# An offset of its own, from 0 to 480 bytes, for the high and low parts of each seven-block weight chunk

## The chip, the cores and the metric

The kernel runs on one core of a Trainium2 chip. The metric is the device time of one execution in microseconds (us); shorter is better.

## The reference

The reference is a small encoder trunk: 512 tokens of width 1024 in float32, two layers, each an attention and an MLP, and a final RMSNorm.

```python
for layer in range(DEPTH):                       # DEPTH = 2
    hn = rmsnorm(h, norm_mix[layer])
    if layer % 2 == 0:
        h = h + hybrid_attention(hn, ...)        # grouped-query and latent heads
    else:
        h = h + neighbourhood_attention(hn, ...) # an 8 x 16 window, learned bias
    h = h + sq_relu_mlp(rmsnorm(h, norm_ffn[layer]), ffn_w_up[layer], ffn_w_down[layer])
return rmsnorm(h, final_norm)

def sq_relu_mlp(h, w_up, w_down):                # 1024 -> 4096 -> 1024
    u = jax.nn.relu(h @ w_up)
    return (u * u) @ w_down
```

The change is in the MLP of both layers.

## The kernel before

*Products in two parts.* TensorE multiplies in a faster float32 form (`fp32r` in the profile) that keeps fewer bits. So each factor is split into a high part (a copy in that form) and a low part (the rest), and a product is three matmuls: high by high, high by low, low by high. The helper `mm3` (lines 614 to 616) does that for plain products with 512 moving columns.

*Seven blocks.* For much of the MLP the kernel saves multiplications by a scheme of Strassen's kind: a 2 x 2 arrangement of blocks is multiplied by seven block products in the place of eight. `seven_chunk` prepares the weights for it: a DMA on SP's queue brings 256 rows by 256 columns (256 KB) into a raw buffer, GpSimd (in a few chunks VectorE) makes sums and differences of its four 128 x 128 blocks (lines 364 to 366), so that seven wanted blocks lie side by side in columns 128 to 1023 of the buffer. Then ScalarE copies these 896 columns into the high part (line 370, tile `whi`), and VectorE subtracts that from the raw columns into the low part (line 371, tile `wlo`). The raw buffer is a slot of the pool `big` (named `a` in the profile) if enough are free, or a tile `raw` of the pool `wp`.

*Its use.* `Seven.run` goes through the chunks of a product. For each of the seven blocks it runs three matmuls of 128 x 128 weights by 256 moving columns (lines 458 to 460): high weights by high input, high weights by low input, low weights by high input. TensorE loads the weights anew for each. The blocks are taken in the order of the list `SEVEN`, block `a` of the chunk being columns 128 a to 128 a + 127 of `whi` and `wlo`.

*Buffers.* `whi` has three buffers of 1024 columns (4096 bytes in each partition), `wlo` four. Plain chunks (`chunk`, lines 224 and 234) and chunks whose low part a DMA sums (`summed_chunk`) take their parts from the same rings.

*Order.* `weights(i)` hands out the parts of chunk i, and before that asks for loads up to five chunks ahead and for the split up to two chunks ahead (`LOAD`, `AHEAD`). So the high and low part of a chunk are written while TensorE works on the chunks before it, and ScalarE may write the next high part as soon as TensorE is through with the chunk three before. GpSimd's sums are held in program order; the rest of the order on the engines follows the program's text and a planner, which knows nothing of offsets within a tile.

*Who reads and writes what.* The moving input of these matmuls (the parts of the seven combinations of the activations) lies in slots of `big`; the output goes to PSUM. Nothing but lines 370, 371 and 458 to 460 touches the high and low parts of a seven-block chunk.

Of the kernel before, what the change touches and what calls it, by code (L numbers as in the profile page):

```python
# [9 lines left out]
F32R = mybir.dt.float32r  # L10
I32 = mybir.dt.int32
AF = mybir.ActivationFunctionType
ALU = mybir.AluOpType
# [5 lines left out]
P = 128  # L19
# [11 lines left out]
def f32(ap):  # L31
    return ap.bitcast(F32)
# [3 lines left out]
def encoder_kernel(ctx: ExitStack, tc: tile.TileContext, ins, out, dbg=None):  # L36
    nc = tc.nc
    PE, ACT, DVE, POOL, SP = nc.tensor, nc.scalar, nc.vector, nc.gpsimd, nc.sync
# [3 lines left out]
    wp = ctx.enter_context(tc.tile_pool(name="wp", bufs=3))  # L42
# [19 lines left out]
    def nm(s):  # L62
        cnt[0] += 1
        return f"{s}_{cnt[0]}"
# [204 lines left out]
    def rows(w, k0, nk):  # L269
        return w[k0 * P : (k0 + nk) * P, :].rearrange("(k p) n -> p k n", p=P)  # L270
# [16 lines left out]
    def begin(i):  # L287
        while begun[0] < len(loaded):
            make = asked[begun[0]][0]
            if make is summed_chunk and begun[0] > i + SUM:  # L290
                break
            if make in (summed_chunk, seven_chunk):
                next(loaded[begun[0]])
            begun[0] += 1
# [55 lines left out]
    SEVEN = [(0, 0), (2, 2), (4, 5), (3, 3), (5, 4), (6, 1), (1, 6)]  # L350

    reserve = [3]

    def seven_chunk(w, k0, c0, eng=None):


        slot = Slot(F32) if len(free) > reserve[0] else None
        raw = slot.t if slot else wp.tile([P, 1024], F32, tag="raw", bufs=4, name=nm("raw"))
        SP.dma_start(raw[:, 0:512].rearrange("p (k n) -> p k n", k=2), rows(w, k0, 2)[:, :, c0 : c0 + 256])
        r = raw.rearrange("p (b n) -> p b n", n=P)  # L360
        yield
        held = (lambda z: z) if eng else tc.keep_in_program_order
        eng = eng or POOL
        held(eng.tensor_tensor(r[:, 6], r[:, 0], r[:, 1], op=ALU.subtract))
        held(eng.tensor_tensor(r[:, 4:6], r[:, 2:3].to_broadcast([P, 2, P]), r[:, 0:7:6], op=ALU.add))  # L365
        held(eng.tensor_tensor(r[:, 7], r[:, 3], r[:, 5], op=ALU.subtract))  # L366
        yield
        hi = wp.tile([P, 1024], F32R, tag="whi", name=nm("whi"))
        lo = wp.tile([P, 1024], F32R, tag="wlo", bufs=4, name=nm("wlo"))
        ACT.activation(hi[:, 0:896], raw[:, 128:1024], AF.Copy)  # L370
        DVE.tensor_tensor(lo[:, 0:896], raw[:, 128:1024], f32(hi[:, 0:896]), op=ALU.subtract)  # L371
        if slot:
            slot.free()
        yield hi, lo, []

    class Seven:
# [63 lines left out]
        def plan(self, w, c0, pairs=None):  # L440

            return [plan(w, pairs[kp] if pairs else 2 * kp, c0, DVE if pairs and c0 and kp in (2, 5) else None,
                         make=seven_chunk)
                    for kp in range(self.np)]
# [1684 lines left out]
```

## Time and profile before

| | us |
|---|---|
| median of 3 runs | 1156.11 |
| lowest and highest | 1155.82, 1156.34 |
| the profiled execution | 1156.15 |
| its span, first to last instruction | 1154.4 |
| TensorE busy in it | 1144.5 |
| VectorE, ScalarE, GpSimd busy | 894.5, 668.7, 597.4 |

"Busy" is the time in which at least one instruction runs on the engine; TensorE's matmuls are pipelined, so that two that overlap count once, and the row of one matmul gives its own length (start to its modelled end), not its pace. The pace is the distance between two starts. PE is TensorE's matmuls, PEld its weight loads, DVE VectorE, ACT ScalarE, POOL GpSimd, SP the queue from which most DMAs are issued. In a group's row stand line, engine, operation, out<-in by the program's names, the shapes, the count, then busy us and mean ns of one, then the engine's idle time before it and what ended most of that. Where one line of the code is asked for, the three numbers are the shortest, the median and the longest in ns, then the first and last start.

### The profile page before, as it was taken

How to read it: one execution, taken by the hardware profiler on the slowest of the kernel's cores; microseconds unless marked ns; L12 is line 12 of the kernel's file. 1: busy time of each engine (PE TensorE's matmuls, PEld its weight loads, DVE VectorE, ACT ScalarE, POOL GpSimd, SP SyncE). 2: the span in 40 equal slices, each digit the busy share in tenths (PEclk: the TensorE clock that was granted, in tenths of full speed). 3: DMA queues.
4: the chain of work that ended last, by engine and by line, in shares of the span. 5: the costliest groups of instructions: out<-in, count | busy, mean ns of one | idle time of the engine just before them, and what ended most of it. 6: DMA issues, size and time to landing. Idle time of an engine off the chain costs nothing.

```text
span 1154.4 us, 20506 instructions
## 1 busy us (share of the span) xinstructions
PE 1144.5 (99%) x7348; PEld 1032.2 (89%) x7348; DVE 894.5 (77%) x1570; ACT 668.7 (58%) x1133; POOL 597.4 (52%) x722
## 2 busy tenths in 40 slices
PE   9999999999999999999999999999999999999997
PEld 8787888888899999899988998988889999989996
DVE  6887998888968777978775667668996877698774
ACT  6676886756256668544454556546543666773334
POOL 4456532327698882378433232321487889436730
PEclk9999999999999999999999999999999999999999
DMA  7322441122523325923585564343343233372332
GB/s 237 109 77 71 120 110 56 64 68 100 180 74 93 91 84 155 268 93 101 153 167 158 150 168 128 117 117 115 114 146 119 75 101 90 72 188 72 120 119 73
DMA packets 118326, 136.06 MB, mean 118 GB/s; under 512 B 9924, under 2 KB 99953, under 8 KB 118225
## 3 DMA queue, kind: packets, MB, share of 16 engines
q1 hardware_dynamic: 110736, 119.83, 34.0%
q0 software_dynamic: 7312, 14.83, 6.7%
q8 instruction: 58, 0.95, 0.3%
q14 instruction: 44, 0.35, 0.1%
q10 hardware_dynamic: 176, 0.10, 0.0%
HBM read 112.70 MB, written 6.29 MB: 103 GB/s over the span
## 4 chain that ended last, share of the span: by engine, by line
PE 93%; issue 4%; DVE 2%; ACT 1%; POOL 0%; POOLq 0%; DVEq 0%; ACTq 0%
PE mm L614 9%; PE mm L615 9%; PE mm L616 9%; PE mm L460 4%; PE mm L459 4%; PE mm L458 4%; PE t L460 3%; PE t L459 3%; PE t L458 3%; PE s L1139 3%; PE o L1127 2%; PE s L460 2%; PE s L459 2%; PE s L458 2%; PE s L616 2%
## 5 line engine op out<-in xcount | busy, mean ns | idle before, releaser
L371 DVE TENSOR_TENSOR wlo<-a,whi 128x896 fp32r<-128x896 f32 x106 | 131.3, 1239 | 59.3 <-ACT whi L370 58.7
L614 PE MATMUL mm<-a,whi 128*128 128x512 f32 x428 | 172.7, 404 | 0.1
L370 ACT ACTIVATE whi<-a 128x896 fp32r<-128x896 f32 x106 | 100.8, 951 | 117.5 <-PE s L459 35.9
L615 PE MATMUL mm<-a,whi 128*128 128x512 f32 x428 | 167.8, 392 | 0.0
L616 PE MATMUL mm<-a,wlo 128*128 128x512 f32 x428 | 167.0, 391 | 0.0
L224 DVE TENSOR_TENSOR wlo<-raw,whi 128x1024 fp32r<-128x1024 f32 (+4 forms) x93 | 105.2, 1138 | 26.7 <-ACT whi L234 26.3
L460 PE MATMUL mm<-a,wlo 128*128 128x256 f32 x430 | 121.7, 283 | 0.0
L459 PE MATMUL mm<-a,whi 128*128 128x256 f32 x430 | 121.7, 283 | 0.0
L458 PE MATMUL mm<-a,whi 128*128 128x256 f32 x430 | 121.7, 283 | 0.0
L234 ACT ACTIVATE whi<-raw 128x1024 fp32r<-128x1024 f32 (+3 forms) x96 | 88.0, 918 | 56.1 <-PE s L615 23.2
L370 ACT ACTIVATE whi<-raw 128x896 fp32r<-128x896 f32 x58 | 55.1, 953 | 86.2 <-PE s L459 26.6
L365 POOL TENSOR_TENSOR a<-a 128x256 f32<-128x256 f32 x104 | 98.6, 948 | 8.2
L616 PEld LDWEIGHTS mm<-a,wlo 128*128 128x128 f32 x428 | 80.4, 188 | 17.1
L366 POOL TENSOR_TENSOR a<-a 128x128 f32<-128x128 f32 x104 | 90.9, 874 | 8.2
L614 PEld LDWEIGHTS mm<-a,whi 128*128 128x128 f32 x428 | 80.5, 188 | 15.5 <-issue 0.5
L1147 POOL TENSOR_SCALAR p<-p,ti 128x512 f32<-128x512 f32 x64 | 48.1, 752 | 88.3 <-DVE ti L1146 67.6
L615 PEld LDWEIGHTS mm<-a,whi 128*128 128x128 f32 x428 | 80.7, 189 | 13.5
L371 DVE TENSOR_TENSOR wlo<-raw,whi 128x896 fp32r<-128x896 f32 x58 | 69.9, 1216 | 28.9 <-ACT whi L370 28.9
L1776 POOL TENSOR_SCALAR p<-p,ti 128x256 f32<-128x256 f32 x64 | 35.5, 567 | 104.6 <-DVE ti L1775 89.8
L460 PE MATMUL t<-a,wlo 128*128 128x256 f32 x312 | 88.3, 283 | 0.0
L459 PE MATMUL t<-a,whi 128*128 128x256 f32 x312 | 88.3, 283 | 0.0
L458 PE MATMUL t<-a,whi 128*128 128x256 f32 x312 | 88.3, 283 | 0.0
(449 smaller groups left out, 3614.9 us busy)
## 6 DMA issues: line engine op xcount, KB each, us to landing
a<-in_ffn_w_up_dram SPq DMA_DIRECT2D x102, 256.0 KB, 2.7
raw<-in_ffn_w_down_dram SPq DMA_DIRECT2D x34, 512.0 KB, 4.3
raw<-in_ffn_w_down_dram SPq DMA_DIRECT2D x56, 256.0 KB, 2.6
raw<-in_od_w_qkv_dram SPq DMA_DIRECT2D x64, 128.0 KB, 3.4
raw<-in_ffn_w_up_dram SPq DMA_DIRECT2D x12, 512.0 KB, 3.8
wlo<-in_ffn_w_down_dram POOLq DMA_DIRECT2D x12, 512.0 KB, 6.0
a<-a SPq DMA_DIRECT2D x17, 256.0 KB, 3.5
bx<-a SPq DMA_DIRECT2D x32, 128.0 KB, 5.6
```

Source lines behind the costliest of these rows:

```text
L224: z = lambda: (eng or DVE).tensor_tensor(to, src, f32(high), op=ALU.subtract)
L234: ACT.activation(hi[:, 0:m], raw[:, 0:m], AF.Copy)
L365: held(eng.tensor_tensor(r[:, 4:6], r[:, 2:3].to_broadcast([P, 2, P]), r[:, 0:7:6], op=ALU.add))
L366: held(eng.tensor_tensor(r[:, 7], r[:, 3], r[:, 5], op=ALU.subtract))
L370: ACT.activation(hi[:, 0:896], raw[:, 128:1024], AF.Copy)
L371: DVE.tensor_tensor(lo[:, 0:896], raw[:, 128:1024], f32(hi[:, 0:896]), op=ALU.subtract)
L458: PE.matmul(o, wh, x[:, 0], start=kp == 0 and n in (0, 1, 3, 5), stop=False, skip_group_check=True)
L459: PE.matmul(o, wh, x[:, 1], start=False, stop=False, skip_group_check=True)
L460: PE.matmul(o, wl, x[:, 0], start=False, stop=kp == self.np - 1, skip_group_check=True)
L614: PE.matmul(o, wh, xh, start=first, stop=False)
L615: PE.matmul(o, wh, xl, start=False, stop=False)
L616: PE.matmul(o, wl, xh, start=False, stop=last)
```

## The change

A helper `places` gives each seven-block chunk two offsets in elements of 4 bytes: both are multiples of 8 elements (32 bytes) from 0 to 120 elements (480 bytes). The high part's goes round through 0, 8, ..., 120 with each chunk; the low part's is the same plus a distance that changes every 16 chunks, modulo 128 elements. The 896 columns of the high and of the low part start at these offsets in their tiles of 1024 columns. Lines 370 and 371 write there, and `Seven.run` takes its blocks from there, since it is handed the slices.

```diff
+    place = [0]
+
+    def places():
+
+        i = place[0]
+        place[0] += 1
+        a = i % 16
+        return 8 * a, 8 * ((a + (0, 1, 2, 4, 8, 3, 6, 12, 15, 14)[i // 16 % 10]) % 16)
 
     def seven_chunk(w, k0, c0, eng=None):
...
         yield
-        hi = wp.tile([P, 1024], F32R, tag="whi", name=nm("whi"))
-        lo = wp.tile([P, 1024], F32R, tag="wlo", bufs=4, name=nm("wlo"))
-        ACT.activation(hi[:, 0:896], raw[:, 128:1024], AF.Copy)
-        DVE.tensor_tensor(lo[:, 0:896], raw[:, 128:1024], f32(hi[:, 0:896]), op=ALU.subtract)
+        a, b = places()
+        hi = wp.tile([P, 1024], F32R, tag="whi", name=nm("whi"))[:, a : a + 896]
+        lo = wp.tile([P, 1024], F32R, tag="wlo", bufs=4, name=nm("wlo"))[:, b : b + 896]
+        ACT.activation(hi, raw[:, 128:1024], AF.Copy)
+        DVE.tensor_tensor(lo, raw[:, 128:1024], f32(hi), op=ALU.subtract)
         if slot:
             slot.free()
         yield hi, lo, []
```

## The prediction

> **What bounds the kernel now.** I read the page first: span, engines, the granted clock and the chain that ended last.
>
> ```profile
> span 1154.4 us, 20506 instructions
> PE 1144.5 (99%) x7348; PEld 1032.2 (89%) x7348; DVE 894.5 (77%) x1570; ACT 668.7 (58%) x1133; POOL 597.4 (52%) x722
> PEclk9999999999999999999999999999999999999999
> PE 93%; issue 4%; DVE 2%; ACT 1%; POOL 0%; POOLq 0%; DVEq 0%; ACTq 0%
> ```
>
> TensorE is busy for 1144.5 of 1154.4 us at a clock that is granted in full, and 93% of the chain is its own work. So the time moves only if a matmul takes another time, or if TensorE has to wait where now it does not.
>
> Next, where do the chunks of the change lie? Each is used by 7 blocks x 3 matmuls (lines 458 to 460). I took the four stretches in which nothing else runs on TensorE, and asked for their busy times.
>
> ```profile
> core 0: us, PE busy (x) PEld busy (x) DVE busy (x) ACT busy (x) POOL busy (x), PEclk, DMA share, GB/s
> 318.07:448.98 130.91, 130.91 (x1093) 130.91 (x1091) 96.34 (x109) 83.90 (x104) 105.96 (x128) 1.00 0.29 85
> 492.65:573.22 80.57, 80.57 (x673) 80.56 (x671) 61.27 (x71) 34.12 (x40) 57.74 (x65) 1.00 0.36 115
> 875.61:1006.52 130.91, 130.91 (x1093) 130.91 (x1091) 94.16 (x108) 82.74 (x103) 106.45 (x128) 1.00 0.27 81
> 1050.49:1120.92 70.43, 70.43 (x588) 70.42 (x587) 53.54 (x66) 28.21 (x33) 45.23 (x51) 1.00 0.37 121
> sum 412.82, PE 412.82 PEld 412.81 DVE 305.31 ACT 228.97 POOL 315.38; mean PE 103.20 PEld 103.20 DVE 76.33 ACT 57.24 POOL 78.84
> ```
>
> The reader sees TensorE without a hole in all four. The chunks are 52 + 32 + 52 + 28 = 164, which is 164 x 21 = 3444 matmuls in 412.82 us: 0.120 us each (412.82 / 3444). That is 36% of the span. The order of time shows the same step, one by one:
>
> ```profile
> 900.08 0.28 PE L458 MATMUL s<-a,whi 128*128 128x256 f32 x1
> 900.20 0.28 PE L459 MATMUL s<-a,whi 128*128 128x256 f32 x1
> 900.32 0.28 PE L460 MATMUL s<-a,wlo 128*128 128x256 f32 x1
> 900.44 0.28 PE L458 MATMUL s<-a,whi 128*128 128x256 f32 x1
> ...
> L458 PEld LDWEIGHTS mm<-a,whi x430: 188/192/192, 317.8 to 1119.8; 128*128 128x128 f32 x144
> L458 PE MATMUL mm<-a,whi x430: 278/283/283, 318.1 to 1120.0; 128*128 128x256 f32 x144
> ```
>
> Starts are 0.12 us apart; the 0.28 us of one matmul overlaps the next. Of 430 weight loads median and longest agree (192 ns), and so do the matmuls' (283 ns). This beat is rigid although ScalarE, VectorE, GpSimd and transfers read and write the same memory beside it, with the shares of the table above. Only one place breaks it:
>
> ```profile
> 497.92 0.35 PE L460 MATMUL s<-a,wlo 128*128 128x256 f32 x1
> 498.10 0.28 PE L458 MATMUL t<-a,whi 128*128 128x256 f32 x1
> 498.22 0.28 PE L459 MATMUL t<-a,whi 128*128 128x256 f32 x1
> ```
>
> A gap of 0.18 us there, and the next is 0.12 again: the beat comes back by itself, for some 0.07 us in all.
>
> **The change, part by part.** No instruction is added, removed or moved: same matmuls, same Copy on ScalarE (L370), same subtraction on VectorE (L371), the same tiles of 1024 columns in the same rings (3 for high, 4 for low), the same DMAs into the raw buffer, on the same queues. What is new is only the byte at which 896 columns start: for the high part 32 x (0 to 15) bytes, for the low part another multiple of 32. The far end, 120 + 896 = 1016, stays inside the 1024. So no order, wait or queue changes, and three prices remain: writing the parts, reading high back, loading weights from them.
>
> *Producers (L370, L371).* Their rows:
>
> ```profile
> L371 DVE TENSOR_TENSOR wlo<-a,whi 128x896 fp32r<-128x896 f32 x106 | 131.3, 1239 | 59.3 <-ACT whi L370 58.7
> L371 DVE TENSOR_TENSOR wlo<-raw,whi 128x896 fp32r<-128x896 f32 x58 | 69.9, 1216 | 28.9 <-ACT whi L370 28.9
> ...
> L371 DVE TENSOR_TENSOR wlo<-a,whi x106: 1076/1208/1672, 311.1 to 1059.2; 128x896 fp32r<-128x896 f32 x106
> L370 ACT ACTIVATE whi<-a x106: 933/955/959, 307.2 to 1058.2; 128x896 fp32r<-128x896 f32 x106
> ...
> ACT whi L370 <- PE s L459: 62.6, 40, 1.6
> ```
>
> L370 is always 933 to 959 ns. L371 goes from 1076 to 1672 ns: it is stretched by whatever runs beside it. No row shows either at another offset, so I bound it: from -151 ns (every L371 at its shortest, 1076, where the mean is now (131.3 + 69.9) / 164 = 1.227 us) to +445 ns (every one at 1672). What covers it: ScalarE waits for TensorE to hand buffers back (62.6 us in 40 waits in the last row), so it runs ahead, not behind. In the stretch from 875.61 to 1006.52 VectorE is idle for 130.91 - 94.16 = 36.75 us over 52 chunks, 0.71 us for each. An L371 longer by 0.445 us still fits, and one shorter brings TensorE nothing. If the cover were gone (over 0.71 us more), each further 0.1 us would cost 16 us over 164 chunks. I take 0.
>
> *Weight loads.* Now every load in these stretches and the moving operand beside it start at one and the same phase: in the program's memory plan the tiles of `big` and `wp` all lie 288 bytes past a multiple of 512, and blocks are 512 and 1024 bytes long. After the change the weights start 0 to 480 bytes further, in steps of 32, and the moving operand stays. The trace has other phases elsewhere: `hT` lies 352 past such a multiple, `ident` 128, `p` 288, `ind` 64. So the transposes of `p` and those of `hT` pair weights and moving operand at distances of 160 and 224 bytes, and the sums with `ind` are at yet another:
>
> ```profile
> L1114 PEld LDWEIGHTS t<-cst,p x256: 138/140/145, 56.9 to 231.6; 128*128 128x128 f32 x128
> L1114 PE MATMUL t<-cst,p x256: 270/272/328, 57.1 to 231.7; 128*128 128x128 f32 x128
> L2010 PEld LDWEIGHTS mm<-cst,hT x12: 138/139/141, 1133.5 to 1140.4; 128*128 128x128 f32 x12
> L2010 PE MATMUL mm<-cst,hT x12: 270/272/273, 1133.8 to 1140.5; 128*128 128x128 f32 x12
> ...
> 121.08 1.04 PE L1114 MATMUL t<-cst,p 128*128 128x128 f32 x8
> 1121.04 0.60 PE L2010 MATMUL s<-cst,hT 128*128 128x128 f32 x4
> ```
>
> Same load (140 and 139 ns), same matmul (272), same step: (1.04 - 0.27) / 7 = 0.11 us and (0.60 - 0.27) / 3 = 0.11 us. These have half the moving columns, and yet 0.11 us: so the pace here is set by the load of 128 columns of weights, and such a load can follow another in 0.11 us. In the long stretches it has 0.12. A load may thus become about 0.01 us longer before anything is seen. A shift by whole multiples of 32 bytes did nothing to it in these rows. One place with another pace:
>
> ```profile
> L731 PEld LDWEIGHTS t<-a,ind x10: 84/86/87, 30.0 to 54.8; 128*6 128x6 f32 x6, 128*4 128x4 f32 x4
> L731 PE MATMUL t<-a,ind x10: 397/397/400, 30.2 to 55.0; 128*6 128x512 f32 x6, 128*4 128x512 f32 x4
> L614 PE MATMUL t<-a,whi x62: 389/389/395, 241.1 to 1030.1; 128*128 128x512 f32 x62
> ```
>
> With weights from `ind` a matmul of 512 columns takes 397 ns against 389, 8 ns more, and with a load of few columns. I take that for the upper end of a disturbed beat: 3444 x 8 ns = +27.6 us. The lower end is that the matmuls run at the loads' pace of the transposes: 3444 x (0.12 - 0.11) = -34 us. Between these ends I take 0, since the transposes are the nearest rows: the same load from two distances, not a nanosecond apart in step; L731 differs in the load's width too.
>
> The sum is 0 + 0. The profiled execution took 1156.15 us (its span 1154.4 and 1.75 around it), the median of the runs is 1156.11; so I forecast 1156.1.
>
> **The rivals.** *Slower: the beat breaks at each chunk.* With another phase for each of 164 chunks the loads could start or end a little later, and the matmuls lose the rigid 0.120 us. For it: the 8 ns of L731, and that no row shows 256-column matmuls at these phases. Against it: the transposes, and the quick recovery at 498 us. Half of the upper end, 4 ns on all 3444, gives +13.8: 1170. It decides as soon as a load needs more than the 0.01 us that it has to spare; 0.7 ns a matmul, or 14 ns a chunk, is already 0.2%.
>
> *Faster: the equal phase costs something now.* Weights and moving operand start together at one phase, and 0.12 us for 256 columns may hold a collision that a spread of phases takes away. All of it gives 1156.1 - 34 = 1122; half of it 1139. Against it: L731 loads 4 to 6 columns at another phase, where there is next to nothing to collide with, and its step is no shorter than that of L614. The Trainium skill ("TensorE: Matmul & The Clock Gate", section "Back-to-back issue gap") gives 262 cycles at full clock for 256 columns, an estimated 109 ns, where this trace measures 120; by that figure the 3444 matmuls would be worth some 37 us less, if the difference came from addresses. The measurement decides what a matmul costs now, and the page does not say that addresses matter.
>
> *Producers fall behind* (slower, too): L371 would have to grow by 0.71 us, more than the spread from 1076 to 1672 that the trace shows. 1160 or more; nothing speaks for it but that no row has these offsets.
>
> **How the numbers follow.** No change 0.82; beat broken 0.09 and producers late 0.02, so slower 0.11; faster 0.07. Some 0.2% (2.3 us) is what a measurement of this kernel can tell from no change. The range is that of the first case, 1153.8 to 1158.6: it leaves out the 0.18 of the others. The likeliest time is that of before.
>
> **What would show it.** Right: in the same four stretches 412.8 us in all, loads of 192 ns and starts 0.12 us apart, L370 within 933 to 959 ns and L371 at 1076 at the least; DVE and POOL may trade waits without effect. Wrong, slower: LDWEIGHTS or MATMUL rows of L458 to L460 with a spread between median and ends, or a sum over 415; or TensorE idle before L460 with L371 as the releaser. Wrong, faster: a sum under 410 with starts 0.11 apart. If steps differ from chunk to chunk, the offset of the chunk should tell which.

## The result: 6 us less, against a forecast of no change

| | before | after |
|---|---|---|
| median, us | 1156.15 (4 runs) | 1150.13 (4 runs) |
| lowest to highest | 1155.82 to 1156.34 | 1149.85 to 1150.46 |
| span of the profiled execution | 1154.4 | 1148.1 |

The ratio is 0.9948 (95% interval 0.9931 to 0.9966): faster by 0.5%. The page after:

```profile
span 1148.1 us, 20506 instructions
PE 1138.1 (99%) x7348; PEld 1025.7 (89%) x7348; DVE 894.2 (78%) x1570; ACT 669.3 (58%) x1133; POOL 602.7 (52%) x722
...
PE 92%; issue 3%; DVE 3%; ACT 1%; POOL 0%; DMA 0%; POOLq 0%; DVEq 0%; ACTq 0%
```

Same instructions, same bound; TensorE is busy for 6.4 us less. The four stretches of the seven-block chunks, from the first matmul of a stretch to the first one behind it, in the stretch table of the kernel after (us, then busy us and count by engine):

```profile
318.47:447.38 128.91, 128.91 (x1093) 128.90 (x1092) 94.84 (x109) 83.93 (x104) 107.95 (x128) 1.00 0.30 86
490.92:570.37 79.45, 79.45 (x673) 79.45 (x672) 59.84 (x70) 34.05 (x40) 58.74 (x64) 1.00 0.36 115
872.70:1001.78 129.08, 129.08 (x1093) 129.08 (x1092) 94.66 (x108) 83.58 (x103) 106.99 (x127) 1.00 0.28 83
1045.32:1114.72 69.40, 69.40 (x589) 69.40 (x588) 54.57 (x66) 28.25 (x33) 44.82 (x51) 1.00 0.38 122
sum 406.84, PE 406.84 PEld 406.83 DVE 303.92 ACT 229.81 POOL 318.51; mean PE 101.71 PEld 101.71 DVE 75.98 ACT 57.45 POOL 79.63
```

Cut in the same way (up to the next matmul's start, so 0.48 us more than in the prediction's table), the kernel before has this:

```profile
sum 413.30, PE 413.30 PEld 413.29 DVE 305.79 ACT 229.21 POOL 315.38; mean PE 103.33 PEld 103.32 DVE 76.45 ACT 57.30 POOL 78.84
```

413.30 - 406.84 = 6.46 us, and the span fell by 6.3: the whole gain lies in these 3444 matmuls, 1.9 ns each. There is no idle time of TensorE in either table, so no wait was removed but for the 0.06 us or so at 498 us, which have no counterpart after. The rows of the matmul's own line and of the producers after:

```profile
L467 PEld LDWEIGHTS mm<-a,whi x430: 187/188/194, 318.2 to 1113.5; 128*128 128x128 f32 x144
L467 PE MATMUL mm<-a,whi x430: 274/281/289, 318.5 to 1113.6; 128*128 128x256 f32 x144
...
L380 DVE TENSOR_TENSOR wlo<-a,whi x106: 1077/1174/1642, 311.6 to 1053.9; 128x896 fp32r<-128x896 f32 x106
L379 ACT ACTIVATE whi<-a x106: 935/954/962, 307.6 to 1052.9; 128x896 fp32r<-128x896 f32 x106
```

The producers are as before, within the spread that they had. The matmul, where median and longest agreed at 283 ns, now spreads from 274 to 289: the rigid beat is gone. Chunk by chunk (21 matmuls, one window each) it reads:

```profile
320.98:323.47 2.49, 2.49 (x24) 2.49 (x22) 1.12 (x1) 0.95 (x1) 2.39 (x3) 1.00 0.00 2
323.47:325.85 2.38, 2.38 (x23) 2.38 (x22) 1.26 (x1) 0.96 (x1) 2.22 (x4) 1.00 0.38 110
325.85:328.38 2.53, 2.53 (x24) 2.53 (x23) 1.42 (x3) 1.23 (x2) 2.37 (x4) 1.00 0.35 104
343.32:345.70 2.38, 2.38 (x23) 2.38 (x22) 1.19 (x2) 2.22 (x3) 1.94 (x3) 1.00 0.42 120
345.70:348.23 2.53, 2.53 (x24) 2.53 (x22) 0.90 (x1) 2.53 (x4) 2.29 (x5) 1.00 0.37 104
```

These are the chunks with both parts at 32, 64, 96, 320 and 352 bytes: 2.38 us at 64 and again at 320, 2.53 at 96 and again at 352 (256 bytes further), whatever ScalarE, VectorE, GpSimd and the transfers do beside them. Before, each took 2.52. From the starts in the trace, in ns a matmul, for chunks with equal offsets of high and low:

```
offset modulo 256   0      32     64     96     128    160    192    224
ns                119.5  118.2  113.6  120.2  118.4  119.7  117.7  118.2
```

### The profile page after: what moved, and what is told of

Same layout as the page of the kernel before. It is cut to its first block, busy times and chain, and to the rows that moved or that the text cites. A ratio compares the mean times of both kernels' runs of the same rounds, so it can differ in the third digit from the quotient of the medians.

```text
span 1148.1 us, 20506 instructions
## 1 busy us (share of the span) xinstructions
PE 1138.1 (99%) x7348; PEld 1025.7 (89%) x7348; DVE 894.2 (78%) x1570; ACT 669.3 (58%) x1133; POOL 602.7 (52%) x722
## 4 chain that ended last, share of the span: by engine, by line
PE 92%; issue 3%; DVE 3%; ACT 1%; POOL 0%; DMA 0%; POOLq 0%; DVEq 0%; ACTq 0%
PE mm L623 9%; PE mm L624 8%; PE mm L625 8%; PE mm L468 4%; PE mm L467 4%; PE mm L469 4%; PE t L468 3%; PE t L469 3%; PE t L467 3%; PE s L1148 3%; PE o L1136 3%; PE s L467 2%; PE s L468 2%; PE s L469 2%; PE s L623 2%
## 5 line engine op out<-in xcount | busy, mean ns | idle before, releaser
L380 DVE TENSOR_TENSOR wlo<-a,whi 128x896 fp32r<-128x896 f32 x106 | 129.7, 1227 | 58.9 <-ACT whi L379 58.4
L379 ACT ACTIVATE whi<-a 128x896 fp32r<-128x896 f32 x106 | 100.8, 951 | 111.8 <-PE s L468 28.5
L379 ACT ACTIVATE whi<-raw 128x896 fp32r<-128x896 f32 x58 | 55.1, 954 | 84.1 <-PE s L468 23.0
L374 POOL TENSOR_TENSOR a<-a 128x128 f32<-128x128 f32 x104 | 90.5, 870 | 8.2
L372 POOL TENSOR_TENSOR a<-a 128x128 f32<-128x128 f32 x104 | 77.2, 743 | 27.8 <-DMA a<-in_ffn_w_up_dram 23.1
L380 DVE TENSOR_TENSOR wlo<-raw,whi 128x896 fp32r<-128x896 f32 x58 | 71.0, 1235 | 24.6 <-ACT whi L379 24.5
L468 PE MATMUL t<-a,whi 128*128 128x256 f32 x312 | 87.5, 281 | 0.0
```

Of the source, the lines that this page charges most:

```text
L379: ACT.activation(hi, raw[:, 128:1024], AF.Copy)
L380: DVE.tensor_tensor(lo, raw[:, 128:1024], f32(hi), op=ALU.subtract)
L468: PE.matmul(o, wh, x[:, 1], start=False, stop=False, skip_group_check=True)
```

## The experiments

Three theories stood ahead of the first runs: *distance* (the pace hangs on the distance, modulo 256 bytes, between the weights that are loaded and the moving operand that is read beside them), *address* (on the weights' place alone), *variety* (a change from chunk to chunk breaks a slow beat). A time with a ratio is the median of four runs; every other time is that of a single run. The kernel before, run beside them, had medians of 1156.05 to 1156.33 us. Paces are taken from the starts in the trace.

**One offset for all: 64 bytes.**

```diff
-        return 8 * a, 8 * ((a + (0, 1, 2, 4, 8, 3, 6, 12, 15, 14)[i // 16 % 10]) % 16)
+        return 16, 16
```

> Every seven-block chunk has its high and its low part at one and the same offset of 64 bytes. Distance theory (the pace of a matmul hangs on the distance, modulo 256 bytes, between the weights that are loaded and the moving operand that is read beside them): all 3444 matmuls at the 113.3 ns that the changed kernel shows for its chunks with 64 and 64, against 120.0 before, so 23 us less: 1133 us. Variety theory (it is the change of offset from chunk to chunk that breaks a slow beat, and a constant one settles at 120 again): 1156 us.

Measured: 1148.39 us, ratio 0.9928 (0.9911 to 0.9945). Neither expectation holds. The first stretch and the sum:

```profile
318.61:447.22 128.61, 128.61 (x1094) 128.61 (x1092) 96.42 (x109) 83.73 (x104) 106.92 (x129) 1.00 0.30 87
...
sum 406.34, PE 406.03 PEld 405.74 DVE 307.68 ACT 228.94 POOL 317.32; mean PE 101.51 PEld 101.43 DVE 76.92 ACT 57.23 POOL 79.33
```

128.61 / 1092 = 117.8 ns, over and over in one pattern of 117 to 119. So a constant offset gives as much as the spread (variety is not needed for a gain), but the same offset that ran at 113.6 in the changed kernel runs at 117.8 here. The distance alone does not fix the pace.

**One offset for all: 96 bytes** (`return 24, 24`).

> The same with a constant offset of 96 bytes. Distance theory: 120.2 ns, as the changed kernel's chunks with 96 and 96 show, so 1156 to 1157 us: an offset as such brings nothing. A theory by which any offset other than 0 is good: about 118 ns, 1149 us. Variety theory: 1156 us too, so this run parts it only from the second.

Measured: 1147.86 us in one run, first stretch 128.13 us:

```profile
318.17:446.30 128.13, 128.13 (x1093) 128.12 (x1092) 96.99 (x109) 83.60 (x104) 107.92 (x128) 1.00 0.31 87
```

117.3 ns, where the chunks at 96 bytes of the changed kernel had 120.2. Again one offset, two paces, so what a chunk finds when it begins may count. In the fourth stretch there is a third pace: behind a wait of TensorE in the 18th chunk the rest runs at 118.7 ns. By its time this run is what the theory of any offset but 0 forecast (1149); the steps of 4 bytes below speak against that one, with 122.8 ns at 48 bytes.

**Everything 64 bytes further.** One line in the kernel before, ahead of the pools:

```diff
     zeros = keep([P, 1], F32, "zeros")
+    keep([P, 16], F32, "pad")
```

> The kernel before with 64 bytes of padding ahead of all the pools, so that weights, moving operands and raw buffers all move by 64 bytes together. Distance theory: nothing changes, 120.0 ns and 1156 us. Address theory (it is the place of the weights in memory itself that counts): 113.3 ns, 1133 us and less, since the plain products' weights move too.

Measured: 1156.22 us, and

```profile
sum 413.26, PE 413.26 PEld 413.24 DVE 305.45 ACT 229.58 POOL 314.61; mean PE 103.31 PEld 103.31 DVE 76.36 ACT 57.39 POOL 78.65
```

The stretches take what they took before, to 0.04 us: the address theory falls. What is left is where weights and moving operands lie towards each other.

**Steps of 4 bytes** (`return i % 64, i % 64`).

> High and low part of chunk i lie at one offset of 4 x (i modulo 64) bytes, so that one profile gives the pace for 64 offsets in steps of 4 bytes. Distance theory: multiples of 32 bytes give again 120.0, 118.2, 113.6, 120.2, 118.4, 119.7, 117.7 and 118.2 ns; between them the pace changes smoothly or in steps of the memory's own width; no value above 125. The time is 1150 us give or take 4. A theory by which 32-byte alignment matters: the multiples of 32 stand out from their neighbours by several ns.

Measured: 1151.03 us. One window for each of six chunks: twice 48, twice 64, twice 96 bytes.

```profile
348.22:350.79 2.57, 2.57 (x23) 2.57 (x22) 2.57 (x4) 1.14 (x3) 2.49 (x3) 1.00 0.26 71
551.08:553.65 2.57, 2.57 (x23) 2.57 (x22) 2.47 (x3) 0.96 (x1) 2.06 (x4) 1.00 0.36 110
358.20:360.58 2.38, 2.38 (x23) 2.38 (x22) 2.07 (x3) 1.29 (x3) 2.29 (x3) 1.00 0.16 57
561.06:563.44 2.38, 2.38 (x23) 2.38 (x22) 1.09 (x1) 0.96 (x1) 2.22 (x3) 1.00 0.76 245
377.85:380.31 2.46, 2.46 (x24) 2.46 (x23) 2.36 (x4) 1.02 (x2) 2.30 (x4) 1.00 0.11 20
882.99:885.45 2.46, 2.46 (x23) 2.46 (x22) 2.36 (x4) 0.96 (x1) 2.30 (x4) 1.00 0.39 107
```

The same offset behind the same neighbour gives the same time, 200 or 500 us apart and with quite other work beside it. Leaving out the first and last chunk of each stretch, all repeats of an offset agree within 0.5 ns. So the pace follows the addresses and what came before, and other work beside it does not show. Over the 64 offsets it goes from 113.3 to 122.8 ns; multiples of 32 bytes do not stand out, and the change is not smooth: 122.8 at 48 bytes, 115.6 at 52. At 32 and 96 bytes I had expected the changed kernel's paces (118.2, 120.2); 118.0 came and 117.1, and at 224 bytes 116.6 for 118.2.

So I formed a second theory, *history*: weights and moving operand are read at the same time and get in each other's way, the delay of one matmul sets the start of the next against its load, and for a given distance there is more than one rhythm (a pattern of steps) that repeats itself.

**The way in.** 64 bytes for all, but the first two chunks of each stretch at 0 and 32, as at the head of the changed kernel:

```diff
-        return 8 * a, 8 * ((a + (0, 1, 2, 4, 8, 3, 6, 12, 15, 14)[i // 16 % 10]) % 16)
+        a = 8 * min(i - max(s for s in (0, 52, 84, 136) if s <= i), 2)
+        return a, a
```

> As the first experiment, 64 bytes for high and low part, but the first two chunks of each of the four stretches have 0 and 32 bytes, as the changed kernel's first stretch has. History theory (for one distance there are several beats that keep themselves up, and the way in decides between them: 113.3 ns behind a chunk at 32 bytes, 117.8 ns behind a plain product's matmuls): the 160 other chunks run at 113.3, but for what follows a wait of TensorE; 21 us less than before, 1135 us, if nothing waits. Theory that a distance has one beat only, and the 113.3 of the changed kernel is a start that dies out: 117.8, 1148 us as in the first experiment.

Measured: 1142.19 us, ratio 0.9878 (0.9860 to 0.9895). First and second stretch, the 50 chunks at 64 bytes of the first, third and fourth stretch, and a row of the waits:

```profile
318.29:442.29 124.00, 124.00 (x1094) 124.00 (x1092) 95.75 (x108) 82.32 (x103) 108.11 (x128) 1.00 0.32 89
486.57:566.28 79.71, 79.66 (x673) 79.38 (x672) 60.80 (x72) 33.90 (x40) 58.86 (x66) 1.00 0.37 115
...
323.28:442.29 119.01, 119.01 (x1053) 119.01 (x1051) 92.87 (x105) 80.41 (x101) 103.35 (x123) 1.00 0.32 88
...
868.57:993.90 125.33, 124.83 (x1093) 124.33 (x1091) 96.72 (x108) 82.34 (x102) 106.52 (x127) 1.00 0.29 84
1038.40:1107.81 69.41, 67.32 (x589) 67.05 (x588) 56.34 (x66) 28.28 (x33) 44.34 (x51) 1.00 0.39 122
...
PE s L470 <- DVE wlo L381: 2.1, 1, 2.1
```

119.01 / 1050 = 113.3 ns for 50 chunks on end: the fast rhythm keeps itself up, with the offset of the first experiment, and only the way in differs. In the second stretch TensorE had to wait inside the second and third chunk (steps of 224, 332 and 226 ns) and came out at 117.8 for the rest. The last row, of the waits, is new: TensorE is now fast enough to wait once for VectorE, 2.1 us. That the way in decides between two paces of one distance is shown; how (the delay of one matmul setting the start of the next) is a picture that no trace shows. The forecast of 1135 was 7 us too low: against 113.3 ns throughout behind the entry, the second stretch lost 3.3 us, the fourth 2.5 (mostly the wait in the row) and the third 1.3 by short waits. (The expectation's 160 other chunks are 156.)

**A later way in** for the second stretch, eight chunks at 0 ahead of it.

```diff
-        return 8 * a, 8 * ((a + (0, 1, 2, 4, 8, 3, 6, 12, 15, 14)[i // 16 % 10]) % 16)
+        a = 8 * min(i - max(s for s in (0, 60, 84, 136) if s <= i), 2)
+        return (0, 0) if 52 <= i < 60 else (a, a)
```

> As the kernel with 64 bytes behind an entry of 0 and 32, but in the second stretch the first eight chunks stay at 0, and the entry comes behind them, since TensorE waited for weights in that stretch's first chunks and came out in the slower beat. History theory: 24 more chunks at 113.3 in the place of 117.8 (2.3 us less), eight at 120.0 (0.4 us more), some 0.4 us of waits less: 1140 us. If the slow beat comes back in that stretch anyway, or the waits only move: 1142.

Measured: 1144.35 us (1140.53 to 1146.69), ratio 0.9896 (0.9870 to 0.9921); the interval overlaps the last one's, and neither 1140 nor 1142 came. In its profile, second and third stretch:

```profile
487.36:565.36 78.00, 77.86 (x674) 77.66 (x672) 61.54 (x70) 33.42 (x39) 57.98 (x64) 1.00 0.38 117
867.66:994.57 126.91, 126.91 (x1093) 126.68 (x1092) 97.44 (x108) 82.41 (x102) 106.33 (x128) 1.00 0.29 83
```

The second stretch won 1.7 us as meant (113.3 behind the entry), but the third fell to 117.8 in its middle, behind waits in three chunks, and lost 1.6. That the other three runs, which have no trace, fell at other places would explain the wide spread, but is not shown. Either way the gain is no stable one.

**Padding between the pools.** The weights' pool moves by 64 bytes against that of the activations; the seven-block chunks have no offset of their own, and the plain products' weights move too.

```diff
+    gap = ctx.enter_context(tc.tile_pool(name="gap", bufs=1))
+    gap.tile([P, 16], F32, tag="gap", name="gap")
     wp = ctx.enter_context(tc.tile_pool(name="wp", bufs=3))
```

> The kernel before with 64 bytes of padding between the pools of the activations and of the weights: the weights of the plain products (512 moving columns) move against their moving operands as well, the seven-block chunks need no offset of their own. Distance theory: the 3444 seven-block matmuls at 113.3 or 117.8 ns, and the steady 226.7 ns of the plain products' matmuls changes too, by up to 7 ns; 1135 to 1148 us. If only what lies in the seven-block chunks' own buffers counted, or the shift of ScalarE's and VectorE's output against their input: 1156 us, since those move together here for the chunks with a raw tile and by 64 for the others.

Measured: 1149.99 us, just above the forecast of 1135 to 1148. Two stretches, the sum of all four, and the plain products' first line:

```profile
321.53:446.75 125.22, 125.22 (x1094) 125.19 (x1092) 96.27 (x109) 83.76 (x104) 105.23 (x126) 1.00 0.32 88
491.09:570.23 79.14, 79.14 (x673) 79.14 (x672) 59.97 (x70) 33.96 (x40) 59.93 (x64) 1.00 0.37 116
...
sum 398.16, PE 397.66 PEld 397.40 DVE 306.10 ACT 228.20 POOL 314.15; mean PE 99.41 PEld 99.35 DVE 76.53 ACT 57.05 POOL 78.54
...
L616 PE MATMUL t<-a,whi x62: 393/394/398, 242.4 to 1025.1; 128*128 128x512 f32 x62
```

The seven-block stretches come to 398.16 us, 15.1 less than before, now without any offset in their buffers; the same two rhythms (113.3, then 117.8 after a disturbance; 79.14 / 672 = 117.8 throughout the second stretch). The plain products' matmul goes from 389 to 394 ns; its steady step, by the starts in the trace, from 226.7 to 233. By the starts, the 2266 matmuls of 512 columns on 128 partitions take 538.6 us here and 528.4 before: 10 us of the gain are lost again. Distance 64 is good for 256 columns and bad for 512.

**The moving operands alone.** Activations by 192 bytes, weights by 256 (`[P, 48]` as the pad, and the gap of the last run), so modulo 256 only the moving operands move.

> Only the activations' pool moves, by 192 bytes, and the weights' pool by 256: modulo 256 the weights lie where they lay before, and their distance to the moving operands is 64 bytes, as in the run with padding between the two pools. Distance theory: the same beats as there, 113.3 and 117.8 ns for the seven-block matmuls, 233 for the plain products', about 1150 us. Theory that only the weights' own place modulo 256 counts: 120.0 and 226.7 ns, 1156 us.

Measured: 1152.85 us.

```profile
492.88:572.02 79.14, 79.14 (x673) 79.14 (x672) 60.59 (x70) 33.97 (x40) 60.12 (x64) 1.00 0.38 116
...
L617 PE MATMUL t<-a,whi x62: 393/394/398, 242.8 to 1028.0; 128*128 128x512 f32 x62
```

Again 117.8 and 394, with 113.3 at the head of the first stretch: the same rhythms with the weights where they were. It is the other operand's place as much. The time is 2.9 us above the last run: the first stretch had more waits, and the third fell into the slow rhythm in its 28th chunk, where that of the last run kept the fast one (401.32 us against 398.16).

**High or low part alone** (`return 8 * a, 0`; then 0 for the high part, the change's offset for the low part).

> The change for the high part alone: its offset goes round from 0 to 480 bytes, the low part starts at 0. Distance theory: each weight load counts by itself, two of three loads are shifted, and the pace lies between 116.5 and 120 ns by chunk, as in the changed kernel's chunks with different offsets; 1150 to 1153 us. Theory that the two parts' distance from each other is what helps or harms: here it differs from chunk to chunk as it does with the change, and the time is that of the change, 1150.

> The change for the low part alone: one of three loads is shifted. Distance theory: still off the beat of 120.0 in most chunks, with less of the gain or as much, 1150 to 1155 us. If the gain needed both parts, or came from the high part's reading by VectorE: 1156 us.

Measured: 1150.94 and 1150.90 us; the sums of the stretches:

```profile
sum 407.64, PE 407.64 PEld 407.63 DVE 306.66 ACT 229.04 POOL 319.66; mean PE 101.91 PEld 101.91 DVE 76.66 ACT 57.26 POOL 79.91
```

```profile
sum 408.25, PE 408.25 PEld 408.23 DVE 305.36 ACT 229.42 POOL 314.47; mean PE 102.06 PEld 102.06 DVE 76.34 ACT 57.36 POOL 78.62
```

Either part gives 5.1 to 5.7 of the 6.46 us. The parts do not add up: moving one load of three is enough to leave the beat of 120.0 in most chunks, and the mean is 118.4 and 118.5 ns, with both parts moved 118.1. The first of the two runs does not part its two theories, which forecast nearly the same time. One offset of 64 bytes for both did that above: no distance between the parts, and 1148.39 us.

**A moving operand that stands still.** The first of the 256 columns is streamed 256 times, with the weights at distance 0 and then 64.

```diff
                     x = self.at(kp, b)
+                    x = [x[:, z, 0:1].to_broadcast([P, 256]) for z in range(2)]
...
```

The three matmuls then read `x[0]` and `x[1]` in the place of `x[:, 0]` and `x[:, 1]`.

> The kernel before, but each seven-block matmul streams the first of its 256 moving columns 256 times (so the MLP's values are others), with weights and moving operand at distance 0. Collision theory (the beat of 120.0 comes from the two streams of reads meeting in the memory as both walk on): with one of them standing still they meet otherwise, the pace changes, and may go as low as the 109 ns of the loads alone in the transposes: 1118 to 1150 us. If where the moving operand is read in the course of a matmul does not matter, only its start: 120.0 ns, 1156 us.

> The same with the weights 64 bytes further, as in the first experiment. Collision theory: the loads walk over all of 512 bytes, twice past any place modulo 256, so the start matters less: within 1 ns of the run at distance 0. If only the starts count: 117.8 or 113.3 ns, 1135 to 1148 us.

Measured: 1136.28 and 1136.80 us. Of the first, the first stretch, the sum of all four and the matmul's row, then the first stretch of the second:

```profile
318.15:440.68 122.53, 122.37 (x1093) 121.98 (x1091) 95.64 (x108) 81.77 (x102) 108.05 (x128) 1.00 0.31 90
...
sum 390.19, PE 386.56 PEld 385.05 DVE 308.74 ACT 225.20 POOL 314.79; mean PE 96.64 PEld 96.26 DVE 77.19 ACT 56.30 POOL 78.70
...
L459 PE MATMUL t<-a,whi x312: 275/275/275, 327.9 to 1083.5; 128*128 128x256 f32 x156
```

```profile
318.44:442.25 123.81, 123.48 (x1093) 122.53 (x1092) 96.78 (x108) 82.09 (x103) 107.02 (x129) 1.00 0.31 89
```

By the starts, both run at 111.7 ns, and both come back to it behind every wait; the stretches are longer than 1092 x 111.7 = 121.98 us only by these waits. One rhythm at both distances tried, and no history: with one of the two streams of reads not walking, the effect is gone. (The time of the second would fit its rival's 1135 to 1148 as well; the pace of 111.7 does not.) The granted clock (0.996 and 0.999 in these runs, 0.998 before) does not account for it.

The trace of the kernel before has the same 111.7 ns in a place that no change here touches. There 128 columns of weights, in plain float32, are loaded for each matmul of a single moving column:

```profile
257.40 0.95 PE L635 MATMUL t<-ones,acc 128*128 128x1 f32 x8
```

By the starts these matmuls step by 112, 112 and 111 ns, over and over (but for the first step of the eight, 26 ns). So the pace with the still operand is that of a stream of loads with next to nothing beside it, and the 8.3 ns on top of it in the kernel before went with the walking operand. That the two streams of reads meet in the memory fits all this, but is argued: an operand of step 0 may also cost less by itself, and 113.3 ns is the least that a walking one reached.

## Why the prediction was wrong, step by step

*What bounds the kernel* held: the stretches of the 3444 matmuls lost 6.46 us, the span 6.3. *No order, wait or queue changes* held as far as TensorE goes, and so did *producers* at 0 (L379 and L380 as before; TensorE waited for neither). The phases of the tiles come from the program's memory plan, which no view here prints; that the chunks' weights and moving operands start at distance 0 fits the runs, since 64 bytes of offset and 64 bytes of padding gave the same two paces.

*Weight loads* failed. The term was put at 0, between -34 and +27.6; it measured -6.46 us. The range of the term held it; the choice within it did not, and the step that failed is "Between these ends I take 0, since the transposes are the nearest rows". The transposes have 128 moving columns, and the prediction itself worked out that their pace of 0.11 us is that of the loads (one moving column steps by 111.7 ns too, L635). A moving stream that is held up by some ns can hide there under the load. So those rows could not show what I asked them, however well they agreed. Their loads also last 140 ns in the rows shown, against 192 in the chunks. What the runs showed in their place: with 256 moving columns, matmuls that load 128 columns of weights each start 113.3 to 122.8 ns apart by the distance of weights and moving operand, and distance 0 runs at 120.0.

*The rigid beat* was read as one that nothing beside it disturbs. That held for ScalarE, VectorE, GpSimd and the transfers, but not for the matmuls' own operands: it is one of several rhythms that keep themselves up. The recovery at 498 us said only that a short wait leads back into it at distance 0; at 64 bytes such a wait can lead into another.

*The rivals.* "Faster: the equal phase costs something now" was the right one, with 0.07; so the chances were too sure. Its mechanism, that the equal phase costs something, held; its size did not: all of it was priced at -34 and half at -17, and the spread of phases brought -6.5, since most distances run at 117 to 120 ns too. Its sign came half: a sum under 410, but starts 0.114 to 0.120 us apart by chunk, not 0.11. With a good distance and way in it was 14 us (1142.19), with a still operand 23 (413.30 - 390.19 in the stretches). I had held L731 against it, where a load of few columns left the step as long; its 397 ns against 389 stay unexplained. The Trainium skill's estimated 109 ns ("TensorE: Matmul & The Clock Gate", "Back-to-back issue gap"; there a figure for an isolated matmul, without its load) spoke for this rival. The runs come near it: of the 11 ns above it, 6.7 went by a distance alone (113.3) and 8.3 with the still operand (111.7). The same page of the Trainium skill ("Step-by-step: what each phase is for") says that "Loading the next tile's weights doesn't steal SBUF read bandwidth from the running matmul". A pace that goes from 113.3 to 122.8 ns with the distance of the two does not fit that, and the measurement decides.

## What to carry to other kernels

Where a row's median and longest agree to the nanosecond, ask whether the value is what the operation needs (try the same operation with an operand that stands still, or look for one with a single moving column), or a rhythm that hangs on where the operands lie. If weights and moving operands share one phase in memory, try a few bytes of padding between their pools, but measure each number of moving columns by itself: 64 bytes won 15 us for 256 columns here and lost 10 of it at 512. A row can bound a cost only where that cost would show: not where something else sets the pace.

## What the hardware showed that was not expected

- With a load of 128 columns of weights for each, matmuls of 256 columns start 113.3 to 122.8 ns apart by the distance of the weights from the moving operand. The paces repeat 256 bytes further, and steps of 4 bytes matter (122.8 at 48, 115.6 at 52).
- With a moving operand that stands still the distance does not matter (0 and 64 bytes tried) and the step is 111.7 ns, the same as with a single moving column (L635).
- One distance has several rhythms (64 bytes: 113.3 and 117.8; 96 bytes: 117.3 and, behind a wait, 118.7; 120.2 in single chunks of the changed kernel). What went before decides between them, and a single wait of TensorE can change it: in the padded kernel's first stretch one step of 149 ns, and 117.8 from there on.
- Shifting weights and moving operands together changes nothing (413.26 us against 413.30).
- Open: whether the two streams of reads meet in the memory, and where, and a distance that leads into the fast rhythm from anywhere. The best kernel here, 64 bytes behind an entry of 0 and 32 (1142.19 us), beats both the kernel before and the change, but a disturbance can throw a stretch back.
